# Eight sample rows multiplied in plain float32 on quarters of the array

## The chip, the cores and the metric

The kernel runs on one core of one Trainium2 chip. The metric is device time in microseconds for one execution; the kernel before takes 990.21 us (median of 3 runs, 989.96 to 990.29).

## The reference

One layer of a decoder trunk, for a prompt of 1024 rows and for 8 separate sample rows, all of width 1024 and float32. Cut to what matters here:

```
proj = rmsnorm(h) @ w_in                       # 1024 x 7168, split into u, v, z_a, x_b, z_b, g_a, g_b
y_a, y_b = ...                                 # gated spatial mixing, gated pooling
m = sigmoid(g_a) * (y_a @ w_pa) + sigmoid(g_b) * (y_b @ w_pb)
h = h + rmsnorm(m @ w_out, post_g)             # the o product, 1024 x 1024
e = p @ w_ple                                  # p is rows x 256, w_ple 256 x 1024
gate = sigmoid(rmsnorm(h, ple_in_g) @ w_pg)    # the gate product, 1024 x 1024
h = h + rmsnorm(gate * e, ple_out_g)
```

It is applied to the prompt and to the 8 sample rows with the same weights. Three products of the sample rows matter here: with `w_ple` (256 x 1024), with `w_out` and with `w_pg` (1024 x 1024 each).

## The kernel before

**Numbers.** Products are made in the format fp32r, at one pass per matmul. To keep float32 accuracy each operand is split in two, a high part (a copy to fp32r) and a low part (the rest); a product is hi*hi + hi*lo + lo*hi. `split` (L350) makes such a pair with one ScalarE copy and one VectorE subtraction.

**Large products.** They go in Strassen's form with seven products (P1 to P7) for a pair of row or column blocks. A step is one such product: 12 matmuls of 128 x 128 weights and 512 moving columns (or 24 of 260). The moving operand has seven parts, B11, B21, B22 and the sums T1 to T4, each held as hi and lo in SBUF. For the last two stages, `outsteps` (with `w_out`, four pairs of seven steps) and `gatesteps` (with `w_pg`), the parts come from weights that were combined and stored in DRAM earlier (`woop`, `wgop`), the tokens are the stationary operand, and the gate's weights already carry the factor `ple_in_g`. The stages before them are the products with `w_in`, `w_pa` and `w_pb`.

**Sample rows.** Up to the merge the 8 sample rows ride along as 8 more columns. From there they have three products of their own. `sample_stationary` (L794) transposes 8 rows with TensorE, and puts hi in columns 0 to 7 and lo in columns 32 to 39 of a stationary block that is zeroed first; `merged_sample` (L1465) does the same for the merged rows, which are transposed already. `sample_matmul` (L783) multiplies such a block by the hi and then the lo part of the weights, so the hi rows come out at PSUM partitions 0 to 7 and the lo rows at 32 to 39 of the tile `sps`; ScalarE copies the latter out and VectorE adds the two. `sample_product` (L1375) uses the parts of `woop` and `wgop`: 4 blocks from B11, 4 from B21 and 8 from T1 and B22, three such sums, and two additions give the left and the right half of the result. That is 16 blocks x 2 matmuls = 32 with `w_out` (`out_sample`, after `outsteps[1][2]`) and 32 with `w_pg` (`embed_gate_sample`, after `gatesteps[1][3]`); the embedding (`embed_sample`, in `embed_rest` after `steps[3]`) has 8 with the split `w_ple`.

**Memory.** SBUF is 46 slots of one size (`SLOTS`, L31), taken by any tile that is made with `slot`. PSUM has three regions of two banks for the large products and two single banks (`bank`, L339) for transposes and the sample rows.

**Order.** A planner (`Planner`, L56) takes all operations in program order, with an estimated duration for each (`duration`, L130), works out when each must be done and when it may start, and writes one order for each engine and for the queues of SyncE and GpSimd, counting free slots and the bytes of transfers. `at(step, f)` puts `f` behind a step in program order; from there the planner may move operations of the other engines and loads, and the order of TensorE's products follows. All engine operations appear in the profile under one line, L299, so groups are told apart by tile names.

Of the kernel before, what the change touches and what calls it, by code (L numbers as in the profile page):

```python
# [9 lines left out]
F32R = mybir.dt.float32r  # L10
# [5 lines left out]
P = 128  # L16
# [3 lines left out]
NS = 8  # L20
# [35 lines left out]
class Planner:  # L56
# [73 lines left out]
    def duration(self, engine, method, out, reads, kwargs):  # L130
        n = out.free_size()
        if engine == "tensor":
            return 0.109 if method == "transpose" else max(0.06, 0.0062 + n / 2268)
        if engine == "vector":
            if method == "tensor_reduce":
                n = reads[0].free_size()
            quick = method in ("tensor_scalar", "tensor_scalar_mul", "tensor_copy")
            quick = quick and self.tags.get(reads[0].tensor.name) in (None, "slot")
            return 0.065 + n * (0.00059 if quick else 0.00105) + (0.06 if method[:8] == "scalar_t" else 0)
        if engine == "scalar":  # L140
            return max(0.09 + n * (0.00101 if out.dtype == U16 else 0.00086), 0.26 if n > 1 else 0) + (0.2 if kwargs.get("accum_out") is not None else 0)
# [164 lines left out]
def hybrid_step(  # L306
# [57 lines left out]
    def mul(out, a, b):  # L364
        nc.vector.tensor_tensor(out=out, in0=a, in1=b, op=ALU.mult)
# [48 lines left out]
    class Operand:  # L414
# [37 lines left out]
        def at(self, what, k):  # L452
            return [part[:, k % 2, :] for part in self.parts[what, k // 2]]
# [278 lines left out]
    def run_stream(steps, first):  # L732
        for s in range(first, len(steps)):
            step = steps[s]
            for f in step.before:
                f()
            if s + FETCH < len(steps):
                for t in range(fetched[0], s + FETCH + 1):
                    if steps[t].loads:
                        steps[t].loads()  # L740
                fetched[0] = max(fetched[0], s + FETCH + 1)
            for t in range(prepared[0], min(len(steps), s + AHEAD + 1)):
                if steps[t].soonest > s:
# [36 lines left out]
        def at(self, n, k):  # L780
            return self.hi[n, k // 2][:, k % 2, :], self.lo[n, k // 2][:, k % 2, :]

    def sample_matmul(terms):  # L783

        ps = bank("sps")
        for n, (st, wh, wl) in enumerate(terms):
            nc.tensor.matmul(ps, st, wh, start=n == 0, stop=False)
            nc.tensor.matmul(ps, st, wl, start=False, stop=n == len(terms) - 1)
        low = slot("slow", (P, HALF))
        nc.scalar.activation(out=low[:NS, :], in_=ps[32 : 32 + NS, :], func=AF.Copy)  # L790
        nc.vector.tensor_tensor(out=low[:NS, :], in0=ps[:NS, :], in1=low[:NS, :], op=ALU.add)
        return low

    def sample_stationary(src, nk, gain=None):  # L794

        st = slot("sst", (P, nk, P), F32R)
        nc.gpsimd.memset(f32(st), 0.0)
        ps = bank("psst").rearrange("p (k t) -> p k t", t=16)
        for k in range(nk):
            nc.tensor.transpose(ps[:, k, :NS], src[:NS, k * P : (k + 1) * P], ident[:NS, :NS])  # L800
        got = ps[:, :nk, :NS]
        if gain is not None:
            mul(smix_s, got, gain.unsqueeze(2).to_broadcast([P, NB, NS]))
            got = smix_s
        split(got, st[:, :, :NS], st[:, :, 32 : 32 + NS])
        return st


# [566 lines left out]
    def sample_product(st, op):  # L1375

        def part(*whats):
            n = 4 * len(whats)
            return sample_matmul([(st[:, k0 + k, :], *op.at(w, k)) for w, k0 in whats for k in range(4)])
        first, left, right = part(("B11", 0)), part(("B21", 4)), part(("T1", 0), ("B22", 4))  # L1380
        for o in (left, right):
            add(o[:NS], first[:NS], o[:NS])
        return left, right

    half = lambda j: slice(j * HALF, (j + 1) * HALF)
    h_of, parts, samples = {}, {}, {}
# [61 lines left out]
    def gate_input(t):  # L1448

        got = h_of.pop(t)  # L1450
        if t == S:
            samples["h"] = sample_stationary(got, NB)
# [12 lines left out]
    def merged_sample():  # L1465
        st = samples["m"] = slot("mst", (P, NB, P), F32R)
        nc.gpsimd.memset(f32(st), 0.0)
        split(big[:, :, SEQ:T], st[:, :, :NS], st[:, :, 32 : 32 + NS])

    def out_sample():  # L1470
        start(S, "hs")
        for j, o in enumerate(sample_product(samples["m"], woop)):
            parts[S].append(square_sum(o[:NS], NS))
            nc.scalar.activation(out=h_of[S][:NS, half(j)], in_=o[:NS], func=AF.Copy)


    ge, e_of = {}, {}
# [5 lines left out]
    def gated(t, c, src):  # L1483
        r = rows(t)
        g = ge[t][:r, c]
        nc.scalar.activation(out=g, in_=src, func=AF.Sigmoid, scale=rin(t))
        mul(g, e_of[t][:r, c], g)
        parts[t].append(square_sum(g, r))
        if len(parts[t]) > 2:
            a, b = parts[t][:2]  # L1490
            both = sm("both")
            nc.vector.tensor_scalar(out=both[:r], in0=a[:r], scalar1=b[:r], scalar2=None, op0=ALU.add)
            parts[t][:2] = [both]
        if t >= NB - 2:
            mul(g, g, gains["out"][:r, c])
# [39 lines left out]

    def embed_gate_sample():
        ge_start(S)
        for j, o in enumerate(sample_product(samples["h"], wgop)):
            gated(S, half(j), o[:NS])
        gate_finish(S)  # L1540


# [20 lines left out]
    at(pbsteps[3][4], lambda: gain_row("post", post_g[0]))  # L1563
    at(outsteps[3][4], lambda: gain_row("out", ple_out_g[0]))
    at(outsteps[0][1], merged_sample)
    at(outsteps[1][2], out_sample)
    at(outsteps[1][4], lambda: out_finish(S))
    at(outsteps[1][6], lambda: gate_norm(S))
    at(outsteps[2][3], lambda: gate_input(S))
    at(gatesteps[1][3], embed_gate_sample)  # L1570
    for i in range(NPAIR):
        nxt = outsteps[i + 1] if i + 1 < NPAIR else gatesteps[0]
        ts = [2 * i + 1, 2 * i]
# [55 lines left out]
        dma(kept["e"][r : r + 2 * P].rearrange("(p i) (n c) -> i p n c", i=2, n=2)[t % 2], e)  # L1629

    def embed_sample():
        st = sample_stationary(praw[2], 2)
        for n in range(2):
            full = sample_matmul([(st[:, k, :], *we.at(n, k)) for k in range(2)])
            dma(kept["e"][SEQ:T, n * HALF : (n + 1) * HALF], full[:NS])


    def begin():
        psl = slot("psamp", (P, PLE))
# [141 lines left out]
```

## Time and profile before

| | us |
|---|---|
| median of 3 runs | 990.21 |
| the profiled execution | 989.81 |
| its span on the core | 988.0 |
| TensorE busy | 974.5 |
| VectorE busy | 797.4 |
| ScalarE busy | 530.2 |
| GpSimd busy | 70.4 |

The span is from the first to the last instruction; the granted clock of TensorE is 0.997 of full speed on average. Transfers moved 174.53 MB, 177 GB/s on average. In the profile, PE is TensorE's matmuls, PEld its weight loads, DVE VectorE, ACT ScalarE, POOL GpSimd and SPq SyncE's queue of transfers. A row such as `sps<-woB11h,mst` names the tile that is written and then those that are read.

### The profile page before, as it was taken

How to read it: one execution, taken by the hardware profiler on the slowest of the kernel's cores; microseconds unless marked ns; L12 is line 12 of the kernel's file. 1: busy time of each engine (PE TensorE's matmuls, PEld its weight loads, DVE VectorE, ACT ScalarE, POOL GpSimd, SP SyncE). 2: the span in 40 equal slices, each digit the busy share in tenths (PEclk: the TensorE clock that was granted, in tenths of full speed). 3: DMA queues.
4: the chain of work that ended last, by engine and by line, in shares of the span. 5: the costliest groups of instructions: out<-in, count | busy, mean ns of one | idle time of the engine just before them, and what ended most of it. 6: DMA issues, size and time to landing. Idle time of an engine off the chain costs nothing. (4 is left out here: it accounts for less than half of the span.)

```text
span 988.0 us, 15969 instructions
## 1 busy us (share of the span) xinstructions
PE 974.5 (99%) x6087; PEld 874.7 (89%) x6087; DVE 797.4 (81%) x1255; ACT 530.2 (54%) x888; POOL 70.4 (7%) x142
## 2 busy tenths in 40 slices
PE   8999999999999999999999999999999999999996
PEld 7789999999999999999999999999999988888885
DVE  6796559787789688989797987697799799779687
ACT  7778988566444433344442333562453365877563
POOL 2100001000000000000000100000000001313111
PEclk9999999999999999999999999999999999999998
DMA  9335553322483253666735085973663452699547
GB/s 335 134 107 112 124 151 128 121 82 74 146 304 131 93 189 114 235 210 211 252 129 192 16 271 204 315 282 130 227 245 120 174 197 60 136 294 361 155 100 201
DMA packets 109290, 174.53 MB, mean 177 GB/s; under 512 B 28631, under 2 KB 68015, under 8 KB 109206
## 3 DMA queue, kind: packets, MB, share of 16 engines
q1 hardware_dynamic: 107118, 166.13, 49.8%
q0 software_dynamic: 2048, 7.37, 4.4%
q8 instruction: 48, 0.79, 0.3%
q14 instruction: 28, 0.23, 0.1%
q10 hardware_dynamic: 48, 0.01, 0.0%
HBM read 114.84 MB, written 53.87 MB: 171 GB/s over the span
## 5 line engine op out<-in xcount | busy, mean ns | idle before, releaser
L299 DVE TENSOR_TENSOR u<-acc,u 128x520 f32<-128x520 f32 (+1 forms) x90 | 62.5, 696 | 31.5 <-PE acc L299 28.4
L299 POOL TENSOR_TENSOR rstd<-ms,mhalf 128x1 f32<-128x1 f32 (+1 forms) x36 | 32.7, 911 | 194.0 <-DVE ms L299 185.4
L299 POOL MEMSET u<- 128x8 f32 x35 | 4.0, 150 | 498.2 <-PE acc L299 238.7
L299 ACT ACTIVATE u<-acc 128x512 f32<-128x512 f32 x39 | 23.3, 598 | 26.3 <-PE acc L299 25.5
L299 ACT ACTIVATE paw<-pas 128x512 fp32r<-128x512 f32 x16 | 10.1, 629 | 31.0 <-DVE pas L299 25.7
L299 ACT ACTIVATE pbw<-pbs 128x512 fp32r<-128x512 f32 x16 | 10.0, 628 | 28.4 <-DVE pbs L299 25.2
L299 DVE TENSOR_TENSOR big<-big 128x1024 f32<-128x1024 f32 (+4 forms) x20 | 23.6, 1218 | 0.0
L299 ACT ACTIVATE big<-mix 128x256 f32<-128x256 f32 x32 | 12.1, 384 | 19.5 <-PE mix L299 17.0
L299 PE MATMUL accm<-qh,wpoolw 128*128 128x260 f32 (+1 forms) x96 | 20.9, 319 | 0.0
L299 ACT ACTIVATE big<-v 128x1024 uint16<-128x1024 uint16 x16 | 18.5, 1174 | 3.8 <-DMA v<-vw 3.8
L299 ACT ACTIVATE zbw<-zbs 128x512 fp32r<-128x512 f32 x16 | 10.1, 628 | 17.2 <-DVE zbs L299 12.0
L299 ACT ACT_TABLE_LOAD x13 | 16.7, 1283 | 4.6 <-PE acc L299 2.1
L299 DVE TENSOR_TENSOR v<-acc,u 128x520 f32<-128x520 f32 (+1 forms) x9 | 6.3, 697 | 15.4 <-PE acc L299 15.4
L299 DVE TENSOR_TENSOR acc<-acc,u 128x512 f32<-128x512 f32 (+1 forms) x16 | 11.2, 700 | 8.8 <-PE acc L299 8.8
L299 ACT ACTIVATE gbw<-gbs 128x512 fp32r<-128x512 f32 x16 | 10.0, 625 | 15.2 <-DVE gbs L299 13.0
L299 ACT ACTIVATE zaw<-zas 128x512 fp32r<-128x512 f32 x16 | 10.1, 629 | 13.5 <-PE acc L299 5.2
L299 PEld LDWEIGHTS accm<-qh,wpoolw 128*128 128x128 f32 x96 | 15.6, 188 | 1.9
L299 DVE TENSOR_TENSOR big<-mix,big 128x256 f32<-128x256 f32 x32 | 12.7, 421 | 5.5 <-ACT big L299 5.1
L299 ACT ACTIVATE gb<-gb 128x1032 f32<-128x1032 f32 (+1 forms) x8 | 6.8, 854 | 19.2 <-DVE gb L299 19.2
L299 ACT ACTIVATE u<-u 128x1032 f32<-128x1032 f32 (+1 forms) x8 | 6.8, 852 | 18.6 <-DVE u L299 18.5
L299 ACT ACTIVATE uw<-us 128x512 fp32r<-128x512 f32 x16 | 10.0, 627 | 12.6 <-DVE us L299 8.3
L299 ACT ACTIVATE vw<-v 128x1024 uint16<-128x1024 uint16 x16 | 16.1, 1045 | 0.5 <-DVE v L299 0.5
(690 smaller groups left out, 3632.5 us busy)
## 6 DMA issues: line engine op xcount, KB each, us to landing
ga<-ga SPq DMA_DIRECT2D x16, 516.0 KB
gb<-gb SPq DMA_DIRECT2D x16, 516.0 KB
ya<-za SPq DMA_DIRECT2D x8, 516.0 KB
yb<-zb SPq DMA_DIRECT2D x8, 516.0 KB
x<-in_x_prompt_dram SPq DMA_DIRECT2D x8, 512.0 KB
vraw<-in_w_in_dram SPq DMA_DIRECT2D x8, 512.0 KB
e<-e SPq DMA_DIRECT2D x8, 512.0 KB
garaw<-in_w_in_dram SPq DMA_DIRECT2D x8, 512.0 KB
```

Of the source, the lines that this page charges most:

```text
L299: getattr(getattr(self.nc, e), method)(*args, **kwargs)
```

## The change

The three products of the sample rows are made in plain float32, without a split. The stationary blocks are 8 columns wide. The weights come as rows straight from the inputs `w_out`, `w_pg` and `w_ple`, in new loads of 128 x 1024, four at a time for two batches each of `w_out` and `w_pg` and two for `w_ple`. Four matmuls stand side by side: with `tile_position=(0, 32 * q)` the q-th uses columns 32q to 32q+31 of the array and writes PSUM partitions 32q to 32q+7. With `w_out` and `w_pg` the four are two halves of the columns by two partial sums over the rows; with `w_ple` two halves by two blocks of rows. A batch of `w_out` or `w_pg` has 8 matmuls, the two batches accumulate in one PSUM tile. `sample_sums` copies three of the four results out with ScalarE and adds twice with VectorE.

Since `w_pg` is not scaled by `ple_in_g` in the input, the gain is multiplied into the stationary block. The embedding's sample product moves from `steps[3]` to `steps[14]`, its loads are at `steps[8]`. The products with `w_out` come in two batches after `outsteps[0][5]` and `outsteps[1][2]`, those with `w_pg` after `gatesteps[1][1]` and `gatesteps[1][5]`. The planner counts 0.3 us for a matmul with a tile position.

```diff
     def duration(self, engine, method, out, reads, kwargs):
         if engine == "tensor":
-            return 0.109 if method == "transpose" else max(0.06, 0.0062 + n / 2268)
+            if method == "transpose":
+                return 0.109
+            return 0.3 if "tile_position" in kwargs else max(0.06, 0.0062 + n / 2268)
...
-    def sample_matmul(terms):
-        ps = bank("sps")
-        for n, (st, wh, wl) in enumerate(terms):
-            nc.tensor.matmul(ps, st, wh, start=n == 0, stop=False)
-            nc.tensor.matmul(ps, st, wl, start=False, stop=n == len(terms) - 1)
-        low = slot("slow", (P, HALF))
-        nc.scalar.activation(out=low[:NS, :], in_=ps[32 : 32 + NS, :], func=AF.Copy)
-        nc.vector.tensor_tensor(out=low[:NS, :], in0=ps[:NS, :], in1=low[:NS, :], op=ALU.add)
-        return low
+    def sample_matmul(ps, groups, first=True, last=True):
+        count = len(groups[0])
+        for k in range(count):
+            for q, terms in enumerate(groups):
+                nc.tensor.matmul(ps[32 * q : 32 * q + NS, :], *terms[k], start=first and k == 0,
+                                 stop=last and k == count - 1, tile_position=(0, 32 * q))
+
+    def sample_sums(ps):
+        parts = [slot("slow", (P, HALF))[:NS] for _ in range(3)]
+        for q, o in enumerate(parts):
+            nc.scalar.activation(out=o, in_=ps[32 * (q + 1) : 32 * (q + 1) + NS, :], func=AF.Copy)
+        add(parts[0], ps[:NS], parts[0])
+        add(parts[2], parts[1], parts[2])
+        return parts[0], parts[2]
...
-        st = slot("sst", (P, nk, P), F32R)
-        nc.gpsimd.memset(f32(st), 0.0)
+        st = slot("sst", (P, nk, NS))
...
-        split(got, st[:, :, :NS], st[:, :, 32 : 32 + NS])
+        if gain is None:
+            nc.vector.tensor_copy(out=st, in_=got)
+        else:
+            mul(st, got, gain.unsqueeze(2).to_broadcast([P, nk, NS]))
...
+    def sample_rows(key, src, b):
+        rawrows[key, b] = [slot(f"{key}rows", (P, D)) for _ in range(4)]
+        for k, r in enumerate(rawrows[key, b]):
+            dma(r, src[(4 * b + k) * P : (4 * b + k + 1) * P, :])
+
+    def sample_product(key, st, b):
+        if b == 0:
+            sample_ps[key] = bank("sps")
+        w = rawrows.pop((key, b))
+        sample_matmul(sample_ps[key], [[(st[:, 4 * b + k], w[k][:, half(j)]) for k in (p, 2 + p)]
+                                       for j in range(2) for p in range(2)], b == 0, b == 1)
...
     at(outsteps[0][1], merged_sample)
+    at(outsteps[0][0], lambda: sample_rows("wo", w_out, 0))
+    at(outsteps[0][5], lambda: sample_product("wo", samples["m"], 0))
+    at(outsteps[0][5], lambda: sample_rows("wo", w_out, 1))
+    at(outsteps[1][2], lambda: sample_product("wo", samples["m"], 1))
     at(outsteps[1][2], out_sample)
...
-    at(gatesteps[1][3], embed_gate_sample)
+    at(gatesteps[0][4], lambda: sample_rows("wg", w_pg, 0))
+    at(gatesteps[1][1], lambda: sample_product("wg", samples["h"], 0))
+    at(gatesteps[1][1], lambda: sample_rows("wg", w_pg, 1))
+    at(gatesteps[1][5], lambda: sample_product("wg", samples["h"], 1))
+    at(gatesteps[1][5], embed_gate_sample)
...
     def embed_sample():
-        st = sample_stationary(praw[2], 2)
-        for n in range(2):
-            full = sample_matmul([(st[:, k, :], *we.at(n, k)) for k in range(2)])
-            dma(kept["e"][SEQ:T, n * HALF : (n + 1) * HALF], full[:NS])
+        st, ps = sample_stationary(praw[2], 2), bank("sps")
+        sample_matmul(ps, [[(st[:, k], werows[k][:, half(n)])] for n in range(2) for k in range(2)])
+        for n, o in enumerate(sample_sums(ps)):
+            dma(kept["e"][SEQ:T, n * HALF : (n + 1) * HALF], o)
...
-        embed_sample()
         we.drop(0)
         we.drop(1)
...
+    at(steps[8], embed_rows)
+    at(steps[14], embed_sample)
```

More of the change, by code (lines that the diff above doesn't have):

```diff
@@ L801, in sample_stationary @@
         got = ps[:, :nk, :NS]
-        if gain is not None:
-            mul(smix_s, got, gain.unsqueeze(2).to_broadcast([P, NB, NS]))
-            got = smix_s
-        split(got, st[:, :, :NS], st[:, :, 32 : 32 + NS])
+        if gain is None:
+            nc.vector.tensor_copy(out=st, in_=got)
+        else:
+            mul(st, got, gain.unsqueeze(2).to_broadcast([P, nk, NS]))
         return st
@@ L1373, in hybrid_step @@
     column_steps("wg", w_pg, [(bflow[7 + 7 * i], bflow[9 + 7 * i]) for i in range(4)])
[L1375 to L1383, printed above, removed]
+    rawrows, sample_ps = {}, {}
+    def sample_rows(key, src, b):
[8 more added lines that the diff above has]
+                                       for j in range(2) for p in range(2)], b == 0, b == 1)
     half = lambda j: slice(j * HALF, (j + 1) * HALF)
@@ L1451, in gate_input @@
         if t == S:
-            samples["h"] = sample_stationary(got, NB)
+            samples["h"] = sample_stationary(got, NB, gvec[:, 2 * NB :])
             return
@@ L1465, in merged_sample @@
     def merged_sample():
-        st = samples["m"] = slot("mst", (P, NB, P), F32R)
-        nc.gpsimd.memset(f32(st), 0.0)
-        split(big[:, :, SEQ:T], st[:, :, :NS], st[:, :, 32 : 32 + NS])
+        st = samples["m"] = slot("mst", (P, NB, NS))
+        nc.vector.tensor_copy(out=st, in_=big[:, :, SEQ:T])
     def out_sample():
         start(S, "hs")
-        for j, o in enumerate(sample_product(samples["m"], woop)):
-            parts[S].append(square_sum(o[:NS], NS))
-            nc.scalar.activation(out=h_of[S][:NS, half(j)], in_=o[:NS], func=AF.Copy)
+        for j, o in enumerate(sample_sums(sample_ps["wo"])):
+            parts[S].append(square_sum(o, NS))
+            nc.scalar.activation(out=h_of[S][:NS, half(j)], in_=o, func=AF.Copy)
     ge, e_of = {}, {}
@@ L1537, in embed_gate_sample @@
         ge_start(S)
-        for j, o in enumerate(sample_product(samples["h"], wgop)):
-            gated(S, half(j), o[:NS])
+        for j, o in enumerate(sample_sums(sample_ps["wg"])):
+            gated(S, half(j), o)
         gate_finish(S)
@@ L1631, in embed_sample, with embed_rows @@
     def embed_sample():
-        st = sample_stationary(praw[2], 2)
-        for n in range(2):
-            full = sample_matmul([(st[:, k, :], *we.at(n, k)) for k in range(2)])
-            dma(kept["e"][SEQ:T, n * HALF : (n + 1) * HALF], full[:NS])
+        st, ps = sample_stationary(praw[2], 2), bank("sps")
+        sample_matmul(ps, [[(st[:, k], werows[k][:, half(n)])] for n in range(2) for k in range(2)])
+        for n, o in enumerate(sample_sums(ps)):
+            dma(kept["e"][SEQ:T, n * HALF : (n + 1) * HALF], o)
+    werows = []
+    def embed_rows():
+        for k in range(2):
+            werows.append(slot("werows", (P, D)))
+            dma(werows[k], w_ple[k * P : (k + 1) * P, :])
     def begin():
```

## The prediction

> **What bounds the kernel now.** I read the page's first lines, then the table of stretches over the whole span, to see where TensorE (PE) ever stands still.
>
> ```profile
> span 988.0 us, 15969 instructions
> PE 974.5 (99%) x6087; PEld 874.7 (89%) x6087; DVE 797.4 (81%) x1255; ACT 530.2 (54%) x888; POOL 70.4 (7%) x142
> ```
>
> ```profile
> 0.00:25.00 25.00, 21.76 (x117) 18.32 (x118) 15.52 (x30) 18.16 (x29) 5.41 (x27) 1.00 0.94 333
> 50.00:75.00 25.00, 25.00 (x159) 22.35 (x158) 23.69 (x30) 18.75 (x28) 0.00 (x0) 1.00 0.30 101
> 75.00:800.00 725.00, 724.79 (x4859) 667.59 (x4858) 588.64 (x936) 360.11 (x585) 23.10 (x63) 1.00 0.53 175
> 800.00:840.00 40.00, 40.00 (x187) 32.93 (x187) 37.92 (x56) 21.40 (x43) 5.05 (x6) 1.00 0.27 71
> 890.00:915.00 25.00, 25.00 (x115) 20.39 (x115) 22.86 (x36) 17.77 (x34) 7.51 (x6) 1.00 1.05 362
> 915.00:940.00 25.00, 25.00 (x117) 20.50 (x116) 17.03 (x28) 12.98 (x27) 3.96 (x5) 1.00 0.51 136
> ```
>
> The columns are the stretch, its length, then busy time of PE, its weight loads, VectorE (DVE), ScalarE (ACT) and GpSimd, the granted clock, the DMA share and GB/s. From 50 us on PE has no hole that matters, at full clock: 0.2 us in the 725 us of the long middle. So in all three places where the sample rows are multiplied, PE time taken out or put in moves the end by the same amount, unless something else becomes late.
>
> What the sample rows cost PE stands in the groups by tile for their PSUM tile `sps`, and in the order of time around one block of them.
>
> ```profile
> 0.00:988.00 988.00, 17.36 (x72) 13.53 (x72) 5.39 (x8) 4.71 (x8) 1.00 0.55 177
> ```
>
> ```profile
> 830.70 0.40 PE L299 MATMUL sps<-woB11h,mst 128*128 128x512 f32 x1
> 830.93 0.39 PE L299 MATMUL sps<-woB11l,mst 128*128 128x512 f32 x1
> ...
> 838.10 0.39 PE L299 MATMUL acct<-woT3h,mw 128*128 128x512 f32 x1
> ```
>
> There are 72 matmuls: 8 in the embedding, 32 with `w_out`, 32 with `w_pg`. The 32 with `w_out` run from 830.70 to 838.10, so one takes 7.40 / 32 = 0.231 us of PE. It shows 0.40 us; the 0.16 us beyond its spacing is overlapped by the next.
>
> **What is removed.** 72 x 0.231 = **16.6 us** of PE, all of it exposed, since no other engine limits these stretches.
>
> **What is added on PE.** Embedding 4 calls, `w_out` 16, `w_pg` 16: 36 calls of 512 columns, in 9 rounds of four, each of the four on 32 other columns of the array. The trace has one plain float32 matmul (not fp32r), the state's sums, and 8-wide weight loads in the sample's transposes:
>
> ```profile
> L299 PEld LDWEIGHTS state<-twice,big x2: 187/188/188, 399.4 to 399.6; 128*128 128x128 f32 x2
> L299 PE MATMUL state<-twice,big x2: 217/246/274, 399.6 to 399.6; 128*128 128x64 f32 x2
> ```
>
> ```profile
> 399.55 0.33 PE L299 MATMUL state<-twice,big 128*128 128x64 f32 x2
> 399.69 0.48 PE L299 MATMUL acc<-xB11h,zbw 128*128 128x512 f32 x1
> ```
>
> ```profile
> L299 PEld LDWEIGHTS vt<-ident,v x8: 83/84/87, 75.1 to 134.0; 128*8 128x8 f32 x8
> L299 PE MATMUL vt<-ident,v x8: 270/271/273, 75.4 to 134.1; 128*8 128x128 f32 x8
> ```
>
> One call in the code became **two** weight loads and two matmuls. Both cover 0.33 us and the second lasts 0.274, so it starts 0.056 us after the first: 0.056 us for 64 columns, 0.448 us for 512. A plain call thus costs 2 x 0.448 = 0.90 us alone, nearly four of the old 0.231. (By the start of the matmul that follows, 0.14 us after the first, it would be 0.07 per half and 1.1 us; that wait contains two 128-wide weight loads, which the new 8-wide ones are not, so I take 0.90.)
>
> No row shows two matmuls on different columns of the array at once. The bounds: if four run as one, a round is 0.90 us, nine are 8.1 us. If nothing overlaps, 36 x 0.90 = 32.3 us. I take four columns at once with each column's own weight loads in the open, because an 8-wide load is a row of the trace (0.084 us) and successive halves of one call use the same 32 columns: a round is 2 x (0.084 + 0.448) = 1.06 us, nine are **9.6 us**. The nearest row is the one that shows what a single column group does in sequence; what I assume beyond it is that the four sequences do not hold each other up.
>
> The Trainium skill, "TensorE: Matmul & The Clock Gate", section "Part 3: Packing small matmuls", gives measured factors of 2.38 for three column tiles and 3.07 for four row tiles at 512 columns; as an estimate from that page, the 32.3 us would become about 10.5 us with the latter, close to my 9.6. No run here shows either.
>
> **Changing the way the array is used.** The five blocks (one embedding, two each for `w_out` and `w_pg`) enter and leave the tiled use, 10 changes. The nearest row is the change from full matmuls to the 8-row transposes and back:
>
> ```profile
> 860.05 0.40 PE L299 MATMUL acct<-woT3h,mw 128*128 128x512 f32 x1
> 860.38 0.66 PE L299 MATMUL psst<-ident,hs 8*128 8x8 f32 x8
> 860.97 0.51 PE L299 MATMUL acct<-woT4h,mw 128*128 128x512 f32 x1
> 861.31 0.39 PE L299 MATMUL acct<-woT4l,mw 128*128 128x512 f32 x1
> ```
>
> 0.33 and 0.34 us stand where 0.23 is usual, 0.11 more each. From nothing to the whole 0.16 us of overlap, ten changes cost 0 to 1.6 us; I take 10 x 0.11 = **1.1 us**.
>
> **What lies beside PE.** The sums change from 8 copies on ACT and 12 additions on DVE (8 out of PSUM, 4 of halves) to 9 copies and 6 additions; at the rows below that is 0.6 us more on ACT and 4.0 us less on DVE. The three splits become one DVE operation each, and the large memsets of `mst` and `sst` go from GpSimd. None of this sets PE's pace: cost 0. If the cover is gone it would be around 98 us, where the embedding's block now falls (`steps[14]`): three copies, 1.8 us of ACT, could delay an evacuation.
>
> ```profile
> L299 ACT ACTIVATE slow<-sps x8: 574/590/593, 69.7 to 945.5; 8x512 f32<-8x512 f32 x8
> L299 DVE TENSOR_TENSOR slow<-sps,slow x8: 670/672/679, 70.9 to 946.8; 8x512 f32<-8x512 f32 x8
> L299 DVE TENSOR_TENSOR slow<-slow,slow x4: 668/672/680, 836.4 to 948.0; 8x512 f32<-8x512 f32 x4
> ```
>
> ```profile
> 90.00:100.00 10.00, 10.00 (x69) 9.16 (x68) 5.92 (x10) 9.12 (x21) 0.00 (x0) 1.00 0.50 94
> ```
>
> **The loads.** New are 18 transfers of 512 KB, 9.4 MB, all on SP's queue, about 0.36 us to issue each. Two (`w_ple`) fall near 80 us and eight (`w_out`) near 800 to 830, where the DMA share is 0.27. The first four of `w_pg` are asked for after `gatesteps[0][4]`, near 906, and used after `gatesteps[1][1]`, near 918; there the share is 1.05 at 362 GB/s. 2.1 MB at that rate are 5.8 us of the DMA engines. Nearest to PE behind them is the last `h` of the prompt, which PE transposes at 918.22:
>
> ```profile
> 904.36 0.89 POOL L299 DMA_DIRECT2D h<-in_x_prompt_dram  x1 [1.46 <-issue]
> ...
> 918.22 1.04 PE L299 MATMUL pht<-ident,h 128*128 128x128 f32 x8
> ```
>
> ```profile
> DMA to landing us min/median/max: 5.3/6.3/9.4
> ```
>
> Issued at 904.36 and landing at latest 9.4 us on, 913.8, it has 4.4 us in hand. If all 5.8 us went in front of it PE would stand 1.4 us. The order is made by the same planner that counts these bytes, and the second four come after 918, at share 0.51; I cost the loads at 0 and keep 0 to 5.8 us for the range. In the queue itself SP waits for other landings, and what stands behind such a wait is late with it:
>
> ```profile
> SPq L299 <- DMA h<-in_x_prompt_dram: 66.2, 6, 40.5
> ```
>
> Four more slots of the 46 are also held between load and product, twice; the trace does not show how many are free.
>
> **Sum.** -16.6 + 9.6 + 1.1 = -5.9 us. The profiled execution took 989.81 us (988.0 of span and 1.8 around it), so 983.9; it lies 0.40 below the median of 990.21, so the forecast against that median is **984.3 us**. With everything at its best (8.1 and 0) it is 981.7.
>
> **Rivals.**
>
> *Two at a time.* If matmuls start strictly in order, the second half of a call waits for its first half on the same columns, and everything behind it waits too; only the second half of one call and the first of the next run together. Then each call costs one half, 36 x 0.448 = 16.1 us, weight loads hidden: 16.1 + 1.1 - 16.6 = +0.6, **990.8 us**. For it: the state's row has two matmuls for one call, and every pair of matmuls in the timeline starts in order. Against it: those rows are all on the whole array. The Trainium skill, "TensorE: Matmul & The Clock Gate", section "Part 3: Packing small matmuls", states that matmuls begin and end in program order without reordering; by that rule this rival would be the outcome. The trace agrees as far as whole-array matmuls go and shows none other.
>
> *Nothing overlaps.* 36 x 0.90 = 32.3 us, + 1.1 - 16.6 = +16.8, **1007.0 us**, slower. The mechanism is the array taking one moving operand at a time; it decides as soon as a call costs more than 0.43 us (where 36 calls and 1.1 us equal 16.6). For it: nothing in the trace runs side by side. Against it: the four moving operands go to separate columns and separate PSUM partitions. This is the change not doing what it says.
>
> *Late rows.* The overlap works, but `w_pg` rows or what queues behind them hold PE near 918: 984.3 + 5.8 = **990.1 us**; with the same loss at `w_out` as well, 995.9. For it: the DMA share of 1.05. Against it: 4.4 us in hand, and PE that had no wait over 0.2 us in the middle of this stream.
>
> **How the numbers follow.** Chances: forecast 0.53, two at a time 0.19, late rows 0.19, nothing overlaps 0.09. About 0.2% (2 us) is what can be told from no change: 988.2 to 992.2. Faster: the forecast's 0.53 and a little of late rows with a small stall, 0.56. Same: most of two at a time and half of late rows, 0.24. Slower: nothing overlaps and the rest, 0.20. The range reaches from the best case, 981.5, over both middling rivals to 993.0, which leaves out the serial case and the worst stalls. The forecast's own range is 981.5 to 987.
>
> **What would show it.** Right: the `sps` group has 72 matmul records of 8-wide weights, a block of 8 calls (2 rounds) takes near 2.1 us from its first start to the next full matmul, records of different columns overlap in time, and PE has no new waits. A block of 3.6 us means two at a time, 7.2 us none. PE waiting for a DMA at `sps` or `pht` near 918 means late rows. The forecast is wrong if the block time and the change of the whole time do not agree; then the rest was moved by the new order of the other engines.

## The result, and the profile after

The changed kernel takes 984.48 us (median of six runs, 982.69 to 986.44), the kernel before, run beside it, 989.79 us (six, 989.06 to 990.29). The ratio is 0.9946 with an interval of 0.9933 to 0.9958: 5.3 us, or 0.5%, faster. The runs of the changed kernel lie 3.7 us apart, those of before 1.2 us. The profiled execution is the slowest of the six, 986.44 us with a span of 984.7 us, and that turns out to matter.

First the page's opening lines and the same stretches as before (stretch, length, busy time of PE, weight loads, DVE, ACT, GpSimd, granted clock, DMA share, GB/s).

```profile
span 984.7 us, 16021 instructions
PE 969.4 (98%) x6087; PEld 864.2 (88%) x6087; DVE 794.9 (81%) x1249; ACT 528.7 (54%) x886; POOL 66.3 (7%) x139
```

```profile
75.00:800.00 725.00, 723.63 (x4839) 666.02 (x4838) 587.24 (x932) 358.54 (x584) 22.61 (x63) 1.00 0.53 176
800.00:840.00 40.00, 39.73 (x205) 30.01 (x204) 37.23 (x54) 19.85 (x37) 2.99 (x4) 1.00 0.56 171
890.00:915.00 25.00, 25.00 (x118) 20.46 (x118) 23.20 (x37) 18.46 (x35) 9.16 (x8) 1.00 1.04 359
```

PE now has a hole of 1.37 us in the long middle, where it had 0.21. The stretch around 890 to 915, which was feared for its DMA share, has none.

Then the five blocks of sample products in the order of time: each `sps` row with the first start of the next full matmul.

```profile
99.17 1.04 PE L301 MATMUL sps<-werows,sst 128*8 128x512 f32 x8
100.14 0.51 PE L301 MATMUL acc<-xT1h,vw 128*128 128x260 f32 x2
...
821.05 1.90 PE L301 MATMUL sps<-worows,mst 128*8 128x512 f32 x16
823.22 0.50 PE L301 MATMUL acct<-woB22h,mw 128*128 128x512 f32 x1 [0.27 <-DVE h L301]
...
834.52 1.90 PE L301 MATMUL sps<-worows,mst 128*8 128x512 f32 x16
836.36 0.50 PE L301 MATMUL acct<-woT3h,mw 128*128 128x512 f32 x1
...
922.79 0.40 PE L301 MATMUL acct<-wgT3h,hw 128*128 128x512 f32 x1
923.12 1.90 PE L301 MATMUL sps<-wgrows,sst 128*8 128x512 f32 x16
924.95 0.50 PE L301 MATMUL acct<-wgT4h,hw 128*128 128x512 f32 x1
925.29 0.39 PE L301 MATMUL acct<-wgT4l,hw 128*128 128x512 f32 x1
...
939.03 1.90 PE L301 MATMUL sps<-wgrows,sst 128*8 128x512 f32 x16
940.86 0.50 PE L301 MATMUL acct<-wgB21h,hw 128*128 128x512 f32 x1
```

A block of 8 calls shows 16 matmul records and takes 1.83 or 1.84 us. One record lasts 0.59 us, so 16 in a row would need 9.5: they overlap, as the prediction asked for. The first `w_out` block takes 2.17, because the matmul behind it waits for DVE. The embedding's 4 calls take 0.97. Together 0.97 + 2.17 + 1.84 + 1.83 + 1.83 = 8.64 us, where 16.6 us stood before. The spacings ahead of a block (922.79 to 923.12, 0.33) and behind its first full matmul (924.95 to 925.29, 0.34) are 0.10 and 0.11 above the usual 0.23, so five blocks cost 5 x 0.21 = 1.05 us for changing the array's use. PE's own saving is 16.6 - 8.64 - 1.05 = **6.9 us**. But the span fell by only 988.0 - 984.7 = 3.3 us. Most of the missing 3.6 us are PE's new waits and a drop of its clock. First the waits of PE that before did not have or had much shorter (waited for; total, times, longest):

```profile
PE acc L301 <- DVE ga L301: 1.4, 1, 1.4
...
PE acct L301 <- DVE ms L301: 0.7, 1, 0.7
```

The largest one, in the order of time, on DVE and PE:

```profile
145.06 0.69 DVE L301 TENSOR_TENSOR gas<-garaw,garaw 128x512 f32<-128x512 f32 x1 [1.40 <-DMA garaw<-in_w_in_dram]
145.68 0.69 DVE L301 TENSOR_TENSOR ga<-acc,u 128x520 f32<-128x520 f32 x1
146.51 0.65 PE L301 MATMUL acc<-xB22h,gaw 128*128 128x260 f32 x2 [1.37 <-DVE ga L301]
```

DVE stands at `gas`, a sum of two raw weight blocks that preparation for a later product needs, until its second block has landed. Behind it in DVE's order stands `ga`, which takes a result out of PSUM, and PE needs that bank. In the kernel before the two stood the other way round:

```profile
145.76 0.70 DVE L299 TENSOR_TENSOR ga<-acc,u 128x520 f32<-128x520 f32 x1 [1.57 <-PE acc L299]
146.37 0.68 DVE L299 TENSOR_TENSOR gas<-garaw,garaw 128x512 f32<-128x512 f32 x1
```

There `ga` went as soon as PE was done. The load itself was not asked for later than before: SP issued the two `garaw` loads from 136.36 us here and from 138.91 us in the kernel before. What changed is which instruction of DVE stands in front of it. No line of the diff touches `ga` or `gas`. The product of the embedding was moved to `steps[14]`, the planner laid out the order of DVE and SP anew, and 47 us behind the moved block two instructions changed places.

Right behind this wait the granted clock falls, in stretches of 5 us:

```profile
145.00:150.00 5.00, 3.63 (x20) 3.57 (x19) 4.93 (x10) 3.65 (x14) 0.86 (x1) 0.66 0.01 3
```

A mean of 0.66 over 5 us is 0.34 x 5 = 1.7 us of full clock lost. The sum for this execution: the wait at 146 costs 1.37 - 0.21 = 1.2, the clock 1.7, and the wait at 967 (0.65 in the timeline) the rest: 3.55 of the 3.6 us. The 0.3 that PE waits for DVE's `h` at 823 is in the block's 2.17 already.

That the sum closes so well is partly chance. Compare when the same matmul starts in both profiles: the changed kernel is 0.4 us ahead at 32 us, before any changed work; it gains 0.8 at the embedding, loses 2.4 at 146, gains 2.9 at `w_out` and 3.4 at `w_pg`, and loses 1.6 behind 950 us. So PE's own saving is confirmed (0.8 + 2.9 + 3.4 = 7.1), the wait and the clock at 146 together cost 2.4 rather than 2.9, and the end costs more than the one wait that the timeline lists there.

### The profile page after: what moved, and what is told of

It is laid out like the page before. It is cut to its first block, busy times and chain, and to the rows that moved or that the text cites. A ratio compares the mean times of both kernels' runs of the same rounds, so it can differ in the third digit from the quotient of the medians.

```text
span 984.7 us, 16021 instructions
## 1 busy us (share of the span) xinstructions
PE 969.4 (98%) x6087; PEld 864.2 (88%) x6087; DVE 794.9 (81%) x1249; ACT 528.7 (54%) x886; POOL 66.3 (7%) x139
## 5 line engine op out<-in xcount | busy, mean ns | idle before, releaser
L301 POOL TENSOR_TENSOR rstd<-ms,mhalf 128x1 f32<-128x1 f32 (+1 forms) x36 | 29.5, 821 | 230.9 <-DVE ms L301 208.2
L301 ACT ACTIVATE big<-mix 128x256 f32<-128x256 f32 x32 | 11.9, 383 | 16.6 <-PE mix L301 15.8
L301 ACT ACTIVATE hw<-hs 128x512 fp32r<-128x512 f32 x16 | 10.0, 627 | 13.3 <-DVE hs L301 8.0
L301 ACT ACTIVATE za<-za 128x1032 f32<-128x1032 f32 (+1 forms) x8 | 6.8, 854 | 17.4 <-DVE za L301 17.3
```

The costliest lines, as they stand in the source:

```text
L301: getattr(getattr(self.nc, e), method)(*args, **kwargs)
```

## The experiments

Each kernel is the changed one with the edit shown. Times are medians with the range of the runs; ratios are to the kernel before, run beside it (989.57, 989.52 and 989.53 us in the three groups in which these runs were made).

### The changed kernel once more

No edit.

> The changed kernel itself, to see how far its times spread beside the others of this group and where PE stands still in another profile. If the 3.7 us between its fastest and slowest time (982.69 to 986.44) come from transfers that land a little earlier or later before DVE, this profile shows other waits than 1.4 us at 146.5 (a load of the gate weights) and 0.8 us near 967, and its time moves by the same amount. If the waits are fixed by the order of work they stand again in the same places with the same length, and the median is again near 984.5.

985.50 us (982.87 to 987.24, six runs), ratio 0.9955 [0.9940, 0.9970]. The profiled execution is this time the fastest, 982.87 with a span of 981.2. It has the same wait of 1.4 us at 146, but neither the clock drop nor the wait at 967:

```profile
145.00:150.00 5.00, 3.76 (x28) 3.67 (x29) 5.00 (x11) 3.66 (x12) 0.86 (x1) 1.00 0.01 2
```

So one and the same program, with one and the same wait, runs at full clock in one execution and at half for part of these 5 us in another. Matched in the same way, 1.5 of the 3.5 us between the two spans arise at this drop, 0.3 at the start and 1.8 behind 950 us. How much of the changed kernel's scatter the drop makes is not shown by two profiles; the kernel before, 1.2 us wide in the first group, is 1.7 to 3.3 us wide in the three later ones.

### Do the four columns carry the gain? All calls on one quarter

```
-                nc.tensor.matmul(ps[32 * q : 32 * q + NS, :], *terms[k], ..., tile_position=(0, 32 * q))
+                nc.tensor.matmul(ps[:NS, :], *terms[k], ..., tile_position=(0, 0))
...
-            nc.scalar.activation(out=o, in_=ps[32 * (q + 1) : 32 * (q + 1) + NS, :], func=AF.Copy)
+            nc.scalar.activation(out=o, in_=ps[:NS, :], func=AF.Copy)
```

> All four calls of a round on the same 32 columns of the array and the same 8 PSUM partitions (their results are added up where they should be apart, so the sample rows come out wrong; all instructions, loads and their counts stay). If the gain rests on four columns groups working at once, a block of 8 calls takes 16 x 0.43 = 6.9 us in place of 1.83, the embedding's 3.4 in place of 0.98, and the kernel 984.5 + 4 x 5.1 + 2.5 = about 1007 us. If instead 8-wide weights alone make plain float32 cheap, the blocks stay at 1.8 us and the time at 984.5.

1006.39 us (1006.19 to 1006.59, two runs), ratio 1.0167 [1.0149, 1.0184]. The first `w_out` block in the order of time:

```profile
822.90 7.03 PE L301 MATMUL sps<-worows,mst 128*8 128x512 f32 x16
829.86 0.50 PE L301 MATMUL acct<-woB22h,mw 128*128 128x512 f32 x1
```

8 calls take 6.96 us instead of 1.83, a factor of 3.8. One call on its own columns is 6.96 / 8 = 0.87 us, which the prediction had worked out as 0.90 from the state's 64-column call. Without the four columns the change would be 17 us slower than before: plain float32 alone loses, side by side it wins. The edit puts all calls on the same columns and on the same PSUM partitions at once; which of the two makes them follow each other is not separated.

### Must the calls be issued round by round? Quarter after quarter

```
-        for k in range(count):
-            for q, terms in enumerate(groups):
+        for q, terms in enumerate(groups):
+            for k in range(count):
```

> The two calls of each column group are issued one behind the other, group after group, where they were issued round by round. If each group of columns works off its own calls and does not hold up the others, a block of 8 calls takes 1.83 us as before and the time stays at 984.5. If matmuls must start in the order of issue (the rival of two at a time), only the last half of one group overlaps the first of the next: 13 halves of 0.43 us, 5.6 us a block, and the kernel takes 984.5 + 4 x 3.8 = about 1000 us. A look-ahead of a few instructions would fall between.

985.34 us (984.97 to 985.94, four runs), ratio 0.9955 [0.9942, 0.9968]: the time of the changed kernel. Now the calls of one quarter follow each other directly in program order, yet the block is as short as before, 835.54 - 833.69 = 1.85 us:

```profile
833.69 1.92 PE L301 MATMUL sps<-worows,mst 128*8 128x512 f32 x16
835.54 0.50 PE L301 MATMUL acct<-woT3h,mw 128*128 128x512 f32 x1
...
922.30 3.56 PE L301 MATMUL sps<-wgrows,sst 128*8 128x512 f32 x16
925.79 0.50 PE L301 MATMUL acct<-wgT4h,hw 128*128 128x512 f32 x1
```

If a matmul had to wait until the one issued ahead of it could start, each quarter's second call would hold up the next quarter, and the block would take the 5.6 us that were expected for that case. It does not: each quarter works off its own calls. The 3.49 us of the first `w_pg` block (925.79 - 922.30) have another cause, since the second block of the same kind in this kernel has the usual length. Its weight loads in the order of time:

```profile
923.96 0.12 PEld L301 LDWEIGHTS sps<-wgrows,sst 128*8 128x8 f32 x6 [0.70 <-DMA wgrows<-in_w_pg_dram]
```

One of the four row blocks had not landed. The six weight loads ahead of this row are, by the order of issue, those of the first quarter's two calls and of the second's first. The third quarter needs rows that the first had used already, and yet it starts only here, together with the call that waited: a call that waits for its load does hold up the quarters issued behind it. The last two of these row blocks had been asked for late, from 913.07, as in the changed kernel from 913.88 (SP's queue, the row of each):

```profile
913.07 3.29 SPq L301 DMA_DIRECT2D wgrows<-in_w_pg_dram  x2
```

```profile
913.88 3.30 SPq L301 DMA_DIRECT2D wgrows<-in_w_pg_dram  x2
```

From the first of these two issues to the block it is about 9 us in both; here the rows cost 3.49 - 1.83 = 1.7 us, in the changed kernel's profile nothing.

### The embedding as before

The embedding's product split into two halves again, at its old place; `w_out` and `w_pg` as changed.

```
...
+        embed_sample()
         we.drop(0)
...
-    at(steps[8], embed_rows)
-    at(steps[14], embed_sample)
```

> Only the products with w_out and w_pg in the new form; the embedding's sample product as it was before, split, at its old place, without the loads of w_ple rows. PE loses 1.86 - 0.98 - 0.19 = 0.7 us of the gain. If the stall of 1.4 us at 146.5 came with the embedding's move (loads in another order on SP's queue), it goes and the time is about 984.5 + 0.7 - 1.2 = 984.0 with less spread. If the stall is due to something else it stays and the time is about 985.2.

986.11 us (983.62 to 987.19, six runs), ratio 0.9957 [0.9943, 0.9970]. The wait at 146 is gone (0.20 us, as in before), so moving the embedding's product had brought it. The time hoped for did not follow: the embedding's 1.86 us are back, 0.6 us are lost to late rows in the first `w_pg` block, and DVE is late at 967 again. The profiled execution, 986.43, was besides late from its start: PE's first wait for DVE's `vw` ends here at 32.50, in the kernel before at 30.87. In the other kernels of this section it ends between 29.8 and 31.6. These 1.6 us lie ahead of all edited work; whether the other five executions have them is not known. The rows of before and of this kernel:

```profile
30.87 0.73 PE L299 MATMUL acc<-xB11h,vw 128*128 128x512 f32 x2 [0.21 <-DVE vw L299]
```

```profile
32.50 0.73 PE L301 MATMUL acc<-xB11h,vw 128*128 128x512 f32 x2 [0.21 <-DVE vw L301]
...
923.47 2.50 PE L301 MATMUL sps<-wgrows,sst 128*8 128x512 f32 x16
925.90 0.50 PE L301 MATMUL acct<-wgT4h,hw 128*128 128x512 f32 x1
...
967.54 0.47 PE L301 MATMUL acct<-wgT1h,hw 128*128 128x512 f32 x1 [0.53 <-DVE ms L301]
```

### What the loads cost: one row block for four

```
-        rawrows[key, b] = [slot(f"{key}rows", (P, D)) for _ in range(4)]
-        for k, r in enumerate(rawrows[key, b]):
+        rawrows[key, b] = [slot(f"{key}rows", (P, D))] * 4
+        for k, r in enumerate(rawrows[key, b][:1]):
```

> Of the four row blocks of a batch only the first is loaded and stands in for all four (the sample rows come out wrong); 12 of the 18 new transfers and 3 slots of each batch fall away, the matmuls stay. If the new loads hold up PE at the w_pg blocks and keep other transfers of the last stages late, the first w_pg block always takes 1.83 us (2.43 and 3.49 were seen in two kernels), the 1 us of waits near 955 to 967 goes, and the time falls from about 985.0 to 983.5 (the wait of 1.4 us near 146 stays). If the loads are hidden, the time stays at 985.0.

984.21 us (982.12 to 985.29, five runs), ratio 0.9944 [0.9932, 0.9957]. With 12 of the 16 loads of `w_out` and `w_pg` gone the time is at most a little below that of the changed kernel (984.48 and 985.50), within its scatter. The loads as a whole are not what holds back the gain. PE still waits 1.3 us at 146, and at the end DVE is late instead of a load, behind the second `w_pg` block:

```profile
930.51 1.90 PE L301 MATMUL sps<-wgrows,sst 128*8 128x512 f32 x16
933.12 0.50 PE L301 MATMUL acct<-wgB22h,hw 128*128 128x512 f32 x1 [0.71 <-DVE ge L301]
```

### `w_pg` as before

The product with `w_pg` by split weights in one block of 32 at `gatesteps[1][3]`; embedding and `w_out` as changed.

```
...
-    at(gatesteps[0][4], lambda: sample_rows("wg", w_pg, 0))
-    at(gatesteps[1][1], lambda: sample_product("wg", samples["h"], 0))
-    at(gatesteps[1][1], lambda: sample_rows("wg", w_pg, 1))
-    at(gatesteps[1][5], lambda: sample_product("wg", samples["h"], 1))
-    at(gatesteps[1][5], embed_gate_sample)
+    at(gatesteps[1][3], embed_gate_sample)
```

> Only the product with w_pg as it was before, split, after gatesteps[1][3], without its loads. PE loses 7.44 - 2 x (1.83 + 0.19) = 3.4 us of the gain. If w_pg's part also brought waits of its own in the last 60 us (0 to 3 us, some 1.5 us on average), the kernel takes 985.0 + 3.4 - 1.5 = 986.9; if its part is free of them, 988.4.

987.24 us (985.91 to 988.57, ten runs), ratio 0.9975 [0.9966, 0.9985]. Put the other way, changing the `w_pg` part too brought 987.24 - 984.48 = 2.8 us by the first six runs of the changed kernel, 1.7 by the second. By PE's work it should bring 32 x 0.231 - 2 x 1.83 - 4 x 0.105 = 3.3 us. The profile of this kernel has no wait of PE in its last 60 us, but a new one of 0.5 us at 585 for DVE's `gb`, which no edit is near to. So the `w_pg` part pays for itself and by the medians gives back 0.5 to 1.6 us of its worth. In the changed kernel's first profile the loss behind 950 us is of that size; in its second there is none.

### The embedding's product two steps earlier

```
-    at(steps[14], embed_sample)
+    at(steps[12], embed_sample)
```

> The embedding's sample product after steps[12] instead of steps[14], nothing else. In the planner's order for SP's queue the two broadcast loads of the LayerNorm rows then stand ahead of the last two transposes again, and not right ahead of the gate weights' load. If the wait of 1.4 us near 146 comes from that order, it goes, and with it the drop of the clock to half for 3.4 us that was seen behind it in two of four profiles: 985.0 - 1.2 - about 0.8 = 983.0. If the wait comes from the embedding's operations themselves, it stays and so does the time.

983.41 us (982.57 to 984.58, five runs), ratio 0.9940 [0.9927, 0.9952]. `ga` stands ahead of `gas` on DVE again, and PE waits 0.2 us there. Its DVE in the order of time:

```profile
144.96 0.70 DVE L301 TENSOR_TENSOR ga<-acc,u 128x520 f32<-128x520 f32 x1 [0.43 <-PE acc L301]
145.57 0.68 DVE L301 TENSOR_TENSOR gas<-garaw,garaw 128x512 f32<-128x512 f32 x1
```

The clock stays full until the last 4 us. A wait of 0.7 us for DVE's `ms` near 965 is still there. The block's length is unchanged (0.98 us), so what gain there is comes from the order. The same kernel run again, to see whether it holds:

> The kernel with the embedding two steps earlier once more, beside the two that build on it: 983.4 again, with the wait near 146 at 0.2 us and no drop of the clock before the end.

983.24 us (982.34 to 984.50, five runs), ratio 0.9938 [0.9925, 0.9950]. Its profiled execution, 982.34, has a span of 980.6, 7.4 us below that of before, and PE stands full in both stretches in question:

```profile
75.00:800.00 725.00, 724.77 (x4854) 666.69 (x4854) 589.26 (x936) 360.12 (x586) 21.81 (x63) 1.00 0.53 177
940.00:965.00 25.00, 25.00 (x110) 20.28 (x109) 21.47 (x36) 14.44 (x31) 5.35 (x6) 1.00 0.71 213
```

Where no wait is added, the whole 6.9 us of PE arrive: of the 7.4 us, 0.3 lie at the start (the wait for `vw` ends at 30.57, before at 30.87). It is the fastest of these five executions. By medians this version is 1.1 to 2.3 us ahead of the changed kernel; five or six runs a side, with overlapping ranges, do not make that difference certain.

### `w_pg` rows and products earlier

With the embedding's product at `steps[12]`:

```
-    at(gatesteps[0][4], lambda: sample_rows("wg", w_pg, 0))
-    at(gatesteps[1][1], lambda: sample_product("wg", samples["h"], 0))
...
+    at(outsteps[2][0], lambda: sample_rows("wg", w_pg, 0))
+    at(outsteps[2][5], lambda: sample_product("wg", samples["h"], 0))
+    at(outsteps[2][5], lambda: sample_rows("wg", w_pg, 1))
+    at(outsteps[3][2], lambda: sample_product("wg", samples["h"], 1))
+    at(outsteps[3][5], embed_gate_sample)
```

> As the kernel with the embedding two steps earlier, and w_pg's rows are loaded and multiplied in the third and fourth pair of the product with w_out (rows after outsteps[2][0] and [2][5], products after outsteps[2][5] and [3][2], the gating after outsteps[3][5]), where DVE is busy 18 of 25 us and away from the stretch with a DMA share of 1.04. If late rows and a full DVE in the last 40 us cost the changed kernel its waits there, they go: 983.0 - 1.5 = 981.5. If the loads only push other transfers of 865 to 915 us back, PE waits there instead and the time is 983 or more.

984.72 us (984.05 to 986.69, five runs), ratio 0.9955 [0.9942, 0.9967]. The end is free of waits, but the loads now stand among those of the gate's weights, and PE waits for both:

```profile
PE acct L301 <- DMA wgB22l<-wgB: 1.1, 1, 1.1
...
PE sps L301 <- DMA wgrows<-in_w_pg_dram: 0.4, 1, 0.4
```

### `w_pg` rows and products later

With the embedding's product at `steps[12]`:

```
...
+    at(gatesteps[1][0], lambda: sample_rows("wg", w_pg, 0))
+    at(gatesteps[1][5], lambda: sample_product("wg", samples["h"], 0))
+    at(gatesteps[1][5], lambda: sample_rows("wg", w_pg, 1))
+    at(gatesteps[2][3], lambda: sample_product("wg", samples["h"], 1))
+    at(gatesteps[2][3], embed_gate_sample)
```

> As the kernel with the embedding two steps earlier, and w_pg's two batches half a pair to a pair later (rows after gatesteps[1][0] and [1][5], products after [1][5] and [2][3], the gating after [2][3]). The loads leave the stretch with a DMA share of 1.04. If the last 60 us lose time to rows and transfers that come late there, the waits near 955 to 965 go and the time falls from 983.4 to about 982.5. If they are due to DVE, which has the sample rows' gating on top of the pairs' own work in these 40 us, the later gating moves the same wait or makes it longer: 983.4 or more.

989.82 us (986.98 to 991.92, eleven runs), ratio 0.9999 [0.9990, 1.0008]: the whole gain is gone, with every block as short as before. The profile shows where. SP's queue, GpSimd, DVE and PE, in the order of time, with what SP waited for between 944 and 950 us (total, times, longest):

```profile
939.52 5.46 SPq L301 DMA_DIRECT2D wgrows<-in_w_pg_dram  x3
949.26 0.34 SPq L301 DMA_DIRECT2D out_dram<-ge  x1
```

```profile
940.07 0.89 POOL L301 DMA_DIRECT2D ge<-h  x1 [1.94 <-DVE hw L301]
```

```profile
SPq L301 <- DMA ge<-h: 4.2, 1, 4.2
```

```profile
952.48 1.29 DVE L301 TENSOR_TENSOR ge<-acct,u 128x512 f32<-128x512 f32 x2 [8.29 <-DMA out_dram<-ge]
```

```profile
953.23 0.79 PE L301 MATMUL acct<-wgB22h,hw 128*128 128x512 f32 x1 [2.90 <-DVE ge L301]
```

DVE is not overloaded at this place: it stands still for 8.29 us, until the store of a finished output has landed and set its buffer `ge` free. Before an output is stored, GpSimd's queue adds `h` to it by a transfer, `ge<-h`. That transfer was issued at 940.07, together with three new row loads of 512 KB on SP's queue (from 939.52), and landed 9 us later, where in the kernel before such a transfer takes 5.3 to 5.8; SP stood 4.2 us for it and issued the store at 949.26. That the row loads are what made it slow is read from the times alone. DVE takes no result out of PSUM in that time, and PE stands 2.90 us. Then the clock falls once more; the stretches show 0.75 and 0.56:

```profile
950.00:955.00 5.00, 2.10 (x6) 1.49 (x5) 2.49 (x4) 1.79 (x3) 0.00 (x0) 0.75 0.97 315
955.00:960.00 5.00, 5.00 (x14) 3.83 (x14) 1.25 (x3) 0.57 (x2) 0.00 (x0) 0.56 0.83 235
```

That is (0.25 + 0.44) x 5 = 3.4 us of clock behind a wait of 2.9. Together this is 6.3 us at most, and the profile has more. It is an execution of 991.05 us, with a span 8.7 us above the 980.6 of the version with the product at `steps[12]`. The last matmul of PE in each, first this kernel, then that one:

```profile
977.57 0.28 PE L301 MATMUL acct<-wgB21h,hw 128*128 128x256 f32 x1
```

```profile
971.94 0.28 PE L301 MATMUL acct<-wgB21h,hw 128*128 128x256 f32 x1
```

PE ends 5.6 us later. From there to the end of the span it is 11.7 us here and 8.7 there, another 3.0 us: DVE, with the gating of the sample rows now among its last work, runs from 972.3 to 985.2 with one pause of 0.5 us. So of the two causes that were expected, late transfers and a full DVE, this execution shows both, the first with about two thirds of the loss.

The changed kernel itself has the beginning of the same chain. ACT, which takes results out of PSUM too, waits in its profile for the same kind of store:

```profile
938.15 0.60 ACT L301 ACTIVATE u<-acct 128x512 f32<-128x512 f32 x1 [4.42 <-DMA out_dram<-ge]
```

PE's wait at 967 follows 29 us later. The links between were not traced one by one, so that the first causes the second is argued, not shown.

### Another estimate in the planner

With the embedding's product at `steps[12]`, a sample matmul at its measured price, 1.83 / 8 = 0.23 us:

```
-            return 0.3 if "tile_position" in kwargs else max(0.06, 0.0062 + n / 2268)
+            return 0.23 if "tile_position" in kwargs else max(0.06, 0.0062 + n / 2268)
```

> As the kernel with the embedding two steps earlier, with the planner counting 0.23 us for a matmul with a tile position, which is what the blocks take (1.83 us for 8), instead of 0.3. If the planner's too long estimate makes it plan DVE's work behind PE too late, the waits of 0.34 us near 820 and 0.8 us near 964 shrink and the time goes to about 982.5. If the order of the work is as good or bad by chance, the time moves by up to 1 us either way around 983.4.

983.83 us (983.61 to 985.22, five runs), ratio 0.9944 [0.9932, 0.9957], the same as with 0.3. A truer estimate does not take the waits away; it puts them elsewhere (0.5 us at `ga`, 0.7 us at `ge`).

## Why the prediction was right, point by point

The forecast was 984.3 us, the median is 984.48, and it was faster by more than the 2 us that can be told apart. The mechanism held on PE, but the closeness is in part luck: two terms were off, in opposite directions.

- **What is removed**, 16.6 us: right. The split product that one experiment kept for `w_pg` still takes 0.23 us a matmul and lies wholly on PE's path.
- **A round of four**, 1.06 us with the weight loads in the open: too dear. Nine rounds took 8.64 us, or 8.3 without the wait behind one block, where 9.6 was taken: 0.92 us a round, close to the lower bound of 0.90. The step that failed is "each column's own weight loads in the open"; the 0.084 us of an 8-wide load do not show between successive halves. In the single records of the block at 834.52 the halves on one column group start 0.43 us apart, where the prediction had 0.084 + 0.448 = 0.53. A round is thus 0.86 us, and the rest of the 0.92 is the way from the last half to the next full matmul. The call alone was right: 0.87 measured against 0.90.
- **Ten changes of the array's use**, 1.1 us: 1.05 measured. The 8-row transposes were the right row to take it from.
- **The other engines**, costed at 0: this is where the prediction was wrong. It named 98 us as the place where cover might fail; nothing happened there. What failed was 47 us later: two instructions of DVE changed places, about 1 us in every profile with the product at `steps[14]`, and in two of these six up to another 1.7 us of clock. The prediction's own sign "PE has no new waits" did not come, and block time and whole time do not agree; for that case its last sentence names "the new order of the other engines", but the sum gives it no price.
- **The loads**, costed at 0: nearly right. The first `w_pg` block lost 0 to 1.7 us, by execution and version, and one load for four saved 0.3 or 1.3 us, by which of the two medians of the changed kernel one takes. The worst that was feared, 5.8 us in front of the last `h`, did not come: the transposes of `h` follow the matmul ahead of them without a wait. But one link was missing: beside the loads the accumulating transfer of an output and its store come late, the store holds a buffer, and DVE or ACT stands at it. With the loads and the gating later the whole gain was lost, most of it in this way.
- **The sum.** PE gained 6.9 us where 5.9 was forecast; the median shows 5.3. So about 1.6 us are lost to waits and clock, and the two errors, +1.0 and -1.6, nearly cancel. Most of the 0.6 that is left is hidden by the kernel before, which measured 989.79 beside the changed one, 0.42 below the 990.21 that the forecast started from. In the second group of six the changed kernel gained 989.57 - 985.50 = 4.1 us, so there 2.8 us are lost.
- **Two at a time**, 990.8: refuted. With the calls in the other order a strict start would have shown, and the block stayed at 1.85 us. The rule of the Trainium skill, "TensorE: Matmul & The Clock Gate", section "Part 3: Packing small matmuls", that matmuls start and end strictly in program order, would give this rival; on separate column groups the trace does not agree with its outcome: 1.83 us for a block issued round by round, where two at a time makes 3.6, and 1.85 issued quarter after quarter, where it makes 5.6.
- **Nothing overlaps**, 1007.0: refuted for the change itself, and confirmed as the price without the four columns, 1006.39.
- **Late rows**, 990.1: right as a mechanism, but 0 to 1.7 us in size, not 5.8.

Left open: what decides in one execution whether the clock falls behind the same wait (it did in two of the six profiles that have a wait of 1.1 to 1.4 us near 146, and in none of the other seven at that place), why the end loses up to 1.6 us, and whether the wait near 967 occurs (it does in the changed kernel's first profile, not in its second).

## What to carry to other kernels

A matmul with 8 stationary columns leaves most of the array idle: here three more ran beside it in the same time. Put four of them on four column groups and price a round by the call alone, with nothing for narrow weight loads and 0.1 us for each change to the tiled use and back. Have the rows of all four there in time, since one late row block holds up the quarters behind it. On a path where PE is full, add to the sum what a new order of the other engines can do: look which instruction that waits for a load stands ahead of one that empties PSUM, and which transfer that must finish before a buffer is free runs beside a new load, since here that took 1 to 3 us, and all of it at worst, of a gain of 7. Before two spans are compared, look where each execution stands ahead of the first changed work: here that differed by up to 2.7 us.

## What the runs showed of the hardware

- Four plain float32 matmuls on four column groups run 3.8 times as fast as on one (1.83 against 6.96 us for 8 calls of 512 columns), and just as fast when the calls of one group are issued directly after each other (1.85 us). The 8-wide weight loads of 0.09 us between successive halves do not show: the halves of one group start 0.43 us apart.
- A call whose load has not landed holds up the column groups issued behind it, though their own rows are there: a wait of 0.70 us made a block of 1.83 us one of 3.49.
- After a wait of PE of only 1.4 us the granted clock can fall: 1.7 us of it were lost behind the wait in the changed kernel's first profile and none in its second; a wait of 2.9 us was followed by a loss of 3.4 us. The Trainium skill, "TensorE: Matmul & The Clock Gate", section "Why this matters for your kernels", advises against gaps above about 3 us. Here shorter ones were enough, though not each time.
